# Two-layer encoder trunk: stores to DRAM issued from GpSimd's queue, pad columns written once

## The chip, the cores and the metric

The kernel runs on one core of a Trainium2 chip. The core has five engines that run their own instruction queues: TensorE (PE), VectorE (DVE), ScalarE (ACT), GpSimd (POOL) and SyncE (SP). SyncE computes nothing; here it issues DMAs. The metric is the device time of one execution in microseconds, the median over runs; lower is better.

## What is computed

Two token groups of 512 x 1024 floats go through two layers with shared weights. Layer 0 is a bidirectional RWKV-7 mixer: seven shifted mixes of the normalised input, projections, and per head a recurrence over time, once forward and once backward:

```python
def step(s, inp):
    r_t, w_t, k_t, v_t, a_t, b_t = inp
    sa = jnp.einsum('bhvk,bhk->bhv', s, a_t)
    s = s * w_t[:, :, None, :] + sa[..., None] * b_t[:, :, None, :] + v_t[..., None] * k_t[:, :, None, :]
    return s, jnp.einsum('bhvk,bhk->bhv', s, r_t)
...
y = ys[0] + ys[1]
...
out = y.reshape(bsz, t, D_INNER).astype(xn.dtype) * jax.nn.silu(z)
return out @ w_o
```

Layer 1 is neighbourhood attention on an 8 x 64 grid (16 heads, a window of 8 rows by 16 columns, learned position bias), gated in the same way. Both layers have RMS norms before and after, and a residual sum. All arithmetic is fp32; the kernel splits each fp32 operand of the large products into a high and a low part and multiplies three times.

## The kernel before, in words

Work is laid out as tiles of 128 features x 512 tokens. In order of time:

- **Prelude** (0 to about 150 us in the profile): norms, the shifted mixes, the first projections (`z` and `k` of group 0). Shifted mixes that are needed later are written to DRAM (`dlv`, `dlk`, `dlr`, `dlz`) from a ring of four tiles, `ls`.
- **Scan** (about 150 to 1090 us): the recurrence runs in chunks of 64 tokens, for eight batches of four heads, eight steps each. `prep` makes the operands of a pair of heads, once for each direction `d`: VectorE writes four parts into the tile `ab` (line 851 in `put`), which has one buffer, and line 870 stores it to the DRAM tensor `dab`. `fetch` later loads one step's operands from there into `cab`, and `V` and `X` from `dvt`. `inverse` builds the chunk inverses (`N`, `NA`, `MT`); `near`, `outer` and `step` are the recurrence; `finish` normalises and gates a batch and stores `dy` from the tile `bv`, into which the next half's `bv` is then loaded. Between them `flow` runs the projections of both groups as a stream: weights into `raw` (three buffers), split into `whi` and `wlo`, inputs into `xr`. The results go through `tmp` (five buffers) to DRAM in `column`; the value projection is also transposed into `vs` (two buffers) and stored to `dvt` by two DMAs a tile.
- **Attention** (about 1090 to 1700 us): projections of both groups, `heads`, the output projection. Here q, k, v and gate go through DRAM as well.
- **End**: `last` computes the second group's output and stores it.

In the scan the order on TensorE, VectorE and ScalarE is written out by a planner: `weave` picks the next piece from a set of threads by a clock (`Clock`) that models each engine, SyncE's queue included. The order on SyncE and GpSimd, and everything outside the scan, is set by the framework's scheduler.

All DMAs, loads and stores, are issued by SyncE through two helpers: `load` (line 309) and `save` (line 306), and directly for the output (lines 1389 and 1455). A queue runs in order: an instruction that waits for a semaphore holds back all behind it.

The tile `e1` holds the exponentials of a chunk with a column of ones in front (`d` = 0) or behind (`d` = 1):

```python
e1 = b("e1", (P, NCH, L + 1))
pad = L * d
gps.memset(e1[:, :, pad:pad + 1], 1.0)
e1v, e0v = e1[:, :, 1 - d:L + 1 - d], e1[:, :, d:L + d]
```

`e1` has one buffer, so this memset on GpSimd waits for VectorE's reads of the tile's last use, and ScalarE's exponential waits for the memset. GpSimd's other work is a few memsets: edges of `xn` and `lm` in the prelude, and `MT` (line 946) in `inverse`, 94 instructions in all.

Of the kernel before, what the change touches and what calls it, by code (L numbers as in the profile page):

```python
# [10 lines left out]
F32 = mybir.dt.float32  # L11
# [7 lines left out]
P = 128  # L19
T = 512  # L20
# [3 lines left out]
NCH = 8  # L24
L = 64
# [24 lines left out]
class Clock:  # L50
# [47 lines left out]
    def note(self):  # L98

        ins = self.nc.cur_bb.bb.instructions  # L100
        end = 0.0
        for j in range(self.seen, len(ins)):
            i = ins[j]
            e = self.ENG.get(str(i.engine).split(".")[-1])
            if e is None or not len(i.outs):
                continue
            end = max(end, self.one(e, i))
        self.seen = len(ins)
        return end
# [104 lines left out]
class Trunk:  # L214
# [88 lines left out]

    def save(self, kind, s, p, src):
        self.sp[kind, s, p] = d = self.dram(f"{kind}{s}{p}", src.shape)
        self.nc.sync.dma_start(d, src)

    def load(self, dst, src):
        self.nc.sync.dma_start(dst, src)
# [277 lines left out]
    def column(self, s, kind, p, ps):  # L587

        nc, sp = self.nc, self.sp
        vt, act = nc.vector, nc.scalar  # L590
        first = lambda e: (e, None, lambda c, n=ps.tensor.name: c.at([n]))
        keep, whole = self.clock.keep, ps.tensor.name
        if kind == "z":

            o, th = self.tmp(), self.tmp()
            if s == 0:
                yield first("D")
                vt.tensor_tensor(o, ps, self.rstd0, op=ALU.mult)
                ps = o
            yield "A" if s == 0 else first("A")  # L600
            keep.add(whole)
            act.activation(th, ps, AF.Tanh, scale=0.5)
            yield "D"
            keep.discard(whole)
            vt.scalar_tensor_tensor(o, th, 1.0, ps, op0=ALU.add, op1=ALU.mult)
            self.save("z", s, p, o)
            return
        yield "A", None, lambda c: max(c.at([ps.tensor.name]), min(c.room(("tmp", id(self.main)), self.NTMP), 1e10))
        o = self.tmp()
        if kind == "k":  # L610
            keep.add(whole)
        act.copy(o, ps)
        self.save(kind, s, p, o)
        if kind == "r":
            self.made.add((kind, s, p))
            return
        if kind == "k":
            yield "A"
            keep.discard(whole)
            sq = self.tmp()  # L620
            act.activation(sq, ps, AF.Square, scale=self.vec("kk", p))
            free, room = self.bank()
            yield "P", free, lambda c: max(room(c), c.at([sq.tensor.name]))
            ss = self.p("pm", (2, T))
            nc.tensor.matmul(ss, self.ssel, sq, start=True, stop=True)
            yield "A"
            row = self.tmp((2, T))
            act.copy(row, ss)
            if p == 0:
                sp["ss", s] = self.dram(f"ss{s}", (16, T))  # L630
            self.load(sp["ss", s][2 * p:2 * p + 2], row)
            self.made.add((kind, s, p))
            if p == NP - 1:
                yield "S", None, lambda c: c.at([sp["ss", s].tensor.name])

                rn = self.tmp((P, 64))
                self.load(rn, sp["ss", s].rearrange("a (b c) -> (a b) c", b=8))
                yield "A"
                act.activation(rn, rn, AF.Sqrt)
                yield "D"  # L640
                vt.tensor_scalar(rn, rn, 1e-12, None, op0=ALU.max)
                vt.reciprocal(rn, rn)
                sp["rn", s, 0] = self.dram(f"rn{s}", (16, T))
                self.load(sp["rn", s, 0].rearrange("a (b c) -> (a b) c", b=8), rn)
                self.made.add(("rn", s))
            return

        if p == 0:

            sp["vt", s] = self.dram(f"vt{s}", (4, 2, NCH // 2, 2, L, 2, 2, HD))  # L650
        yield "A"
        back = self.tmp()
        act.copy(back, o[:, ::-1])
        for d in range(2):
            free, room = self.bank()
            yield "P", free, lambda c: max(room(c), c.at([back.tensor.name]))
            vp = self.p("pm")
            for m in range(4):
                nc.tensor.transpose(vp[:, m * P:(m + 1) * P], (back if d else o)[:, m * P:(m + 1) * P], self.ident)
            yield "A", None, lambda c: max(c.at([vp.tensor.name]), c.room(("vs", id(self.main)), self.NVS))  # L660
            vs = self.t("vs", (P, 4, P), self.NVS)
            act.copy(vs, vp.rearrange("p (m c) -> p m c", m=4))
            for j in range(2):
                self.load(
                    sp["vt", s][p // 2, j, :, :, :, d, p % 2].rearrange("m h t c -> t (m h) c"),
                    vs[64 * j:64 * j + 64].rearrange("t m (h c) -> t (m h) c", h=2))
        self.made.add((kind, s, p))
# [90 lines left out]
    def prep(self, s, p):  # L758

        nc, sp = self.nc, self.sp  # L760
        vt, gps, act = nc.vector, nc.gpsimd, nc.scalar
# [38 lines left out]
        for d in range(2):  # L800
# [22 lines left out]
            else:  # L823
                vt.tensor_tensor_scan(cw[:, ::-1], self.scan[1][:, ::-1], u[:, ::-1], 0.0, op0=ALU.mult, op1=ALU.add)
            yield "A"
            e1 = b("e1", (P, NCH, L + 1))
            pad = L * d
            gps.memset(e1[:, :, pad:pad + 1], 1.0)
            e1v, e0v = e1[:, :, 1 - d:L + 1 - d], e1[:, :, d:L + d]
            act.activation(e1v, c3(cw), AF.Exp, scale=-CDEC)  # L830
            e2 = b("u")
            act.activation(e2, cw, AF.Exp, scale=CDEC)


            act.copy(wc[:, d, g] if d == 0 else wc[:, d, g, ::-1], e1[:, :, L - pad])
            ck = max(self.clock.room(("ab", id(self.pp)), 1), 0.0)
            ab = b("ab", (P, NCH, 4, L), 1)

# [28 lines left out]
            yield "D"  # L867
            put(1, mul, c3(kp), c3(e2))
            kps.append(kp)
            self.load(sp["ab", s, pb][:, :, d, g, :].rearrange("c p a -> p c a"), ab.rearrange("p c a t -> p c (a t)"))  # L870

            def gram(ab=ab, d=d):

# [498 lines left out]
    def out1(self, s):  # L1372
        nc = self.nc
# [11 lines left out]
        for k, h in enumerate(hs):  # L1385
            x = self.load(self.t("xr", bufs=self.NXR), self.sp["x1", s, k])
            nc.vector.scalar_tensor_tensor(h, h, self.vec("post1", k), rstd, op0=ALU.mult, op1=ALU.mult)
            (nc.vector if k % 2 else nc.vector).tensor_tensor(h, h, x, op=ALU.add)
            nc.sync.dma_start(self.a["y"][s][k * P:(k + 1) * P, :], h)
            yield  # L1390

    def by_token(self):
# [12 lines left out]
    def last(self):  # L1405
# [27 lines left out]
        for c in range(2):  # L1433
            cs = slice(c * T, c * T + T)
            for m in range(4):
# [12 lines left out]
                if c:  # L1448
# [3 lines left out]
                    vt.reciprocal(r, r)  # L1452
                    for j in range(2):
                        vt.scalar_tensor_tensor(hs[j, m], hs[j, m], r, xt[j], op0=ALU.mult, op1=ALU.add)
                        nc.sync.dma_start(self.a["y"][1][ms, j * T:j * T + T], hs[j, m])


    def stream(self):
# [53 lines left out]
    def scan_phase(self, mid):  # L1512
# [2 lines left out]
        self.mrx = t("mrx", (P, 2, 2, L))  # L1515
        for d in range(2):
            self.nc.vector.tensor_copy(self.mrx[:, d], self.mr[d].unsqueeze(1).broadcast_to([P, 2, L]))
        self.MTb = [t(f"MT{j}", (P, 32, 2, 32)) for j in range(2)]
        self.nM = 0

# [260 lines left out]
```

## Time and profile before

| | |
|---|---|
| median of 3 runs | 1752.39 us (1751.27 to 1755.62) |
| span of the profiled execution | 1748.0 us |
| difference of the two | 4.4 us |
| TensorE busy | 1604.4 us, 92% of the span |
| VectorE busy | 1213.3 us, 69% |
| ScalarE busy | 973.6 us, 56% |
| GpSimd busy | 24.1 us, 1% |
| DMA | 336.26 MB, mean 192 GB/s, of them 105.51 MB written to DRAM |

The profiled execution's own time is its span and what lies around it; of the three runs only the whole time is known, so the span stands beside their median.

How to read it: in the windows, each engine's number is its busy time in the stretch, with the count of instructions. In a table of waits, "A <- B: t, n, m" says that A stood idle for t us in n cases, at most m us, until B was done. SPq is SyncE's queue; a row of its timeline has the start, the time for which the DMA instructions occupied the queue, line, and destination <- source. A bracket at the end of a timeline row gives the idle time before it and what ended it. The DMA list gives the size and the median time from issue to landing.

### The profile page before, as it was taken

What the parts mean: (1) busy time and instruction counts of PE and PEld (TensorE: products, weight loads), DVE (VectorE), ACT (ScalarE), POOL (GpSimd) and SP (SyncE); (2) the same over time, 40 slices, a digit from 0 to 9 for tenths busy, and PEclk for the clock granted to TensorE, in tenths of its full rate; (3) what the DMA queues carried; (4) which work ended last, traced back from release to release, by engine and by line L of the source; (5) the groups of instructions that cost most, each with busy time, mean ns of one, the idle gap of its engine ahead of it and who ended that gap; (6) DMA issues with size and microseconds to landing.
All of it is one profiled execution on the core that took longest, in us unless ns stands there. A gap on an engine that the chain in (4) does not pass through costs nothing.

```text
span 1748.0 us, 46203 instructions
## 1 busy us (share of the span) xinstructions
PE 1604.4 (92%) x18816; PEld 1228.1 (70%) x18816; DVE 1213.3 (69%) x2645; ACT 973.6 (56%) x1964; POOL 24.1 (1%) x94
## 2 busy tenths in 40 slices
PE   7999788998999996898998988999999999999998
PEld 6766665765766674666766676787777788777776
DVE  8976588788888569796888857423556686555564
ACT  5444665666664565666666444333556664555462
POOL 0000000000000000000000000000000000000000
PEclk9989988999999997999999989999999999999999
DMA  5436677685666657777556766554555347545552
GB/s 201 163 115 211 219 266 221 204 269 190 213 198 209 198 172 254 221 213 251 186 187 216 247 200 201 186 204 139 175 184 166 103 132 262 174 155 158 162 175 97
DMA packets 240821, 336.26 MB, mean 192 GB/s; under 512 B 53697, under 2 KB 119361, under 8 KB 240609
## 3 DMA queue, kind: packets, MB, share of 16 engines
q1 hardware_dynamic: 240608, 333.31, 58.7%
q8 instruction: 148, 2.42, 0.6%
q14 instruction: 65, 0.52, 0.1%
HBM read 227.71 MB, written 105.51 MB: 191 GB/s over the span
## 4 chain that ended last, share of the span: by engine, by line
PE 61%; DVE 17%; DMA 8%; ACT 7%; issue 5%; SPq 1%; DVEq 0%; ACTq 0%
PE pg L404 6%; PE pg L405 6%; PE pg L406 6%; PE pm L738 5%; PE pm L739 5%; PE pm L740 5%; PE pm L1331 3%; DVE etmp L928 2%; PE po L1359 2%; PE pt L1346 2%; DVE N L929 2%; PE pf L1030 2%; DVE ab L851 2%; DMA cab<-dab 2%; PE zy L404 1%
## 5 line engine op out<-in xcount | busy, mean ns | idle before, releaser
L738 PE MATMUL pm<-act,whi 128*128 128x512 f32 x608 | 268.6, 442 | 17.9 <-ACT whi L699 8.0
L739 PE MATMUL pm<-act,whi 128*128 128x512 f32 x608 | 246.8, 406 | 19.0 <-DVE act L723 18.7
L740 PE MATMUL pm<-act,wlo 128*128 128x512 f32 x608 | 245.1, 403 | 2.3 <-DVE wlo L701 2.3
L404 PE MATMUL pg<-act,whi 128*128 128x512 f32 x448 | 181.6, 407 | 0.4 <-ACT whi L353 0.4
L405 PE MATMUL pg<-act,whi 128*128 128x512 f32 x448 | 178.4, 398 | 0.0
L406 PE MATMUL pg<-act,wlo 128*128 128x512 f32 x448 | 177.9, 397 | 0.0
L354 DVE TENSOR_TENSOR wlo<-raw,whi 128x512 fp32r<-128x512 f32 x156 | 107.0, 688 | 93.3 <-ACT whi L353 80.5
L353 ACT CAST whi<-raw 128x512 fp32r<-128x512 f32 x156 | 96.2, 618 | 131.6 <-PE pg L405 62.5
L701 DVE TENSOR_TENSOR wlo<-raw,whi 128x512 fp32r<-128x512 f32 x152 | 103.2, 686 | 84.4 <-ACT whi L699 83.1
L738 PEld LDWEIGHTS pm<-act,whi 128*128 128x128 f32 x608 | 117.7, 194 | 54.9 <-ACT whi L699 9.3
L739 PEld LDWEIGHTS pm<-act,whi 128*128 128x128 f32 x608 | 118.3, 195 | 44.9 <-DVE act L723 24.3
L740 PEld LDWEIGHTS pm<-act,wlo 128*128 128x128 f32 x608 | 118.3, 195 | 30.2 <-DVE wlo L701 4.4
L699 ACT CAST whi<-raw 128x512 fp32r<-128x512 f32 x152 | 93.0, 618 | 73.0 <-PE pm L739 55.8
L404 PEld LDWEIGHTS pg<-act,whi 128*128 128x128 f32 x448 | 84.3, 188 | 24.5 <-issue 9.1
L405 PEld LDWEIGHTS pg<-act,whi 128*128 128x128 f32 x448 | 84.3, 188 | 18.4 <-issue 3.5
L406 PEld LDWEIGHTS pg<-act,wlo 128*128 128x128 f32 x448 | 84.2, 188 | 18.2 <-issue 2.2
L929 DVE TENSOR_TENSOR N<-etmp,N 128x30 f32<-128x30 f32 (+14 forms) x240 | 79.8, 332 | 8.2
L1342 ACT ACTIVATE sb<-sb,mx 128x256 f32<-128x256 f32 x128 | 64.1, 502 | 37.6 <-DVE mx L1341 37.1
L928 DVE TENSOR_TENSOR etmp<-N 128x30 f32<-128x30 f32 (+14 forms) x240 | 78.7, 328 | 4.4
L1339 DVE CUSTOM_DVE_ANT_0 sb<-pm,bias 128x256 f32<-128x256 f32 x128 | 50.3, 421 | 45.1 <-PE pm L1331 34.2
L1045 ACT COPY Tm<-pf 128x512 f32<-128x512 f32 x56 | 32.8, 586 | 86.5 <-DVE R L1038 86.5
L1030 PE MATMUL pf<-cab 64*64 64x128 f32 (+1 forms) x2048 | 71.8, 279 | 9.3 <-DMA cab<-dab 6.8
(369 smaller groups left out, 3372.1 us busy)
## 6 DMA issues: line engine op xcount, KB each, us to landing
dab<-ab SPq DMA_DIRECT2D x32, 1024.0 KB, 5.8
cab<-dab SPq DMA_DIRECT2D x64, 512.0 KB, 4.5
raw<-in_w_in_dram SPq DMA_DIRECT2D x128, 256.0 KB, 3.0
bias<-in_rpb_dram SPq DMA_DIRECT2D x32, 384.0 KB, 4.3
raw<-in_w_z_dram SPq DMA_DIRECT2D x32, 256.0 KB, 4.4
dz<-tmp SPq DMA_DIRECT2D x32, 256.0 KB, 2.3
raw<-in_w_k_dram SPq DMA_DIRECT2D x32, 256.0 KB, 3.2
dk<-tmp SPq DMA_DIRECT2D x32, 256.0 KB, 2.2
```

Source lines behind the costliest of these rows:

```text
L353: self.nc.scalar.copy(hi, src)
L354: (eng or self.nc.vector).tensor_tensor(lo, src, hi.bitcast(F32), op=ALU.subtract)
L404: nc.tensor.matmul(ps, hi, x[k][0], start=(k == 0), stop=False)
L405: nc.tensor.matmul(ps, hi, x[k][1], start=False, stop=False)
L406: nc.tensor.matmul(ps, lo, x[k][0], start=False, stop=(k == KT - 1))
L701: nc.vector.tensor_tensor(lo, raw.pop(h), hi.bitcast(F32), op=ALU.subtract)
L738: nc.tensor.matmul(ps, hi[:, at], xh, start=(k == 0), stop=False)
L739: nc.tensor.matmul(ps, hi[:, at], xl, start=False, stop=False)
L740: nc.tensor.matmul(ps, lo[:, at], xh, start=False, stop=(k == KT - 1))
L928: vt.tensor_tensor(tv, N[:, q + 1:, q:q + 1].broadcast_to([P, n, q]), N[:, q:q + 1, :q].broadcast_to([P, n, q]), op=ALU.mult)
L929: vt.tensor_tensor(N[:, q + 1:, :q], tv, N[:, q + 1:, :q], op=ALU.add)
L1030: end = nc.tensor.matmul(f[half(a), h, 0, d, g] if st.last else f[half(a), h, :, d, g], ab[half(h), d, g, 2 * e[d] + a], rt if st.last els ...
```

## The change

Every store to DRAM goes through a new helper `store`, which issues it from GpSimd's queue: `save`, the sums `ss` and `rn`, the transposed values, the operands `ab`, and both outputs. Loads stay on SyncE's. The planner's clock still counts every DMA as SyncE's, whichever engine issues it. The tile `e1` becomes one fixed tile with a column of ones at each end, written once ahead of the scan; the exponentials always lie in columns 1 to 64, and each direction reads a view shifted one way or the other. The 32 memsets in `prep` go.

```diff
-            e = self.ENG.get(str(i.engine).split(".")[-1])
+            e = "S" if "DMA" in type(i).__name__.upper() else self.ENG.get(str(i.engine).split(".")[-1])
...
     def save(self, kind, s, p, src):
         self.sp[kind, s, p] = d = self.dram(f"{kind}{s}{p}", src.shape)
-        self.nc.sync.dma_start(d, src)
+        self.store(d, src)
+
+    def store(self, dst, src):
+        self.nc.gpsimd.dma_start(dst, src)
...
-            self.load(sp["ss", s][2 * p:2 * p + 2], row)
+            self.store(sp["ss", s][2 * p:2 * p + 2], row)
...
-                self.load(
+                self.store(
                     sp["vt", s][p // 2, j, :, :, :, d, p % 2].rearrange("m h t c -> t (m h) c"),
...
-            e1 = b("e1", (P, NCH, L + 1))
-            pad = L * d
-            gps.memset(e1[:, :, pad:pad + 1], 1.0)
-            e1v, e0v = e1[:, :, 1 - d:L + 1 - d], e1[:, :, d:L + d]
+            e1 = self.e1
+            e1v, e0v = e1[:, :, 1:L + 1], e1[:, :, 2 * d:L + 2 * d]
...
-            act.copy(wc[:, d, g] if d == 0 else wc[:, d, g, ::-1], e1[:, :, L - pad])
+            act.copy(wc[:, d, g] if d == 0 else wc[:, d, g, ::-1], e1[:, :, 1 if d else L])
...
-            self.load(sp["ab", s, pb][:, :, d, g, :].rearrange("c p a -> p c a"), ab.rearrange("p c a t -> p c (a t)"))
+            self.store(sp["ab", s, pb][:, :, d, g, :].rearrange("c p a -> p c a"), ab.rearrange("p c a t -> p c (a t)"))
...
-            nc.sync.dma_start(self.a["y"][s][k * P:(k + 1) * P, :], h)
+            self.store(self.a["y"][s][k * P:(k + 1) * P, :], h)
...
+        self.e1 = self.t("e1", (P, NCH, L + 2), 1, F32, self.pp)
+        for pad in (0, L + 1):
+            self.nc.gpsimd.memset(self.e1[:, :, pad:pad + 1], 1.0)
```

(`rn` and the second output change in the same way.) SyncE goes from 1176 rows to 845. The order on TensorE, VectorE and ScalarE is the same in the scan but for a few rows of VectorE and ScalarE at its start; it differs in neighbouring rows in the prelude and in attention.

The first place is SyncE's queue in the scan, in the value projection of group 0, ahead of a load of a step's operands (`cab`; `V`, `X` and `r` are loads too, `dab`, `dvt` and `dks` stores). Before:

```order
L309 DMA V_2749<-dvt_642_2506 128x256
L309 DMA X_2755<-dvt_642_2506 64x2x128
L309 DMA V_2752<-dvt_642_2506 128x256
L309 DMA dab_626_2463<-ab_2733 128x8x256
L309 DMA raw_2791<-in_w_v_dram 128x512
L309 DMA dvt_642_2506<-vs_2799 64x8x64 x2
L309 DMA dvt_642_2506<-vs_2871 64x8x64 x2
L309 DMA cab_441_1698<-dab_466_1778 128x1024
L309 DMA V_2904<-dvt_642_2506 128x256
```

The same place now:

```order
L312 DMA X_2746<-dvt_639_2501 64x2x128
L312 DMA raw_2782<-in_w_v_dram 128x512
L312 DMA V_2743<-dvt_639_2501 128x256
L312 DMA X_2926<-dvt_639_2501 64x2x128
L312 DMA cab_442_1701<-dab_467_1781 128x1024
L312 DMA V_2895<-dvt_639_2501 128x256
L312 DMA r_2972<-dr_525_2020 128x512
```

The operand store and four stores of transposed values no longer stand between the weight load and the `cab` load.

The second place is where those stores stand, around the operand stores of the next pair of heads. On SyncE before (`dv` and `dvt` are the values as projected and transposed, `rb` a load for `prep`):

```order
L306 DMA dv_658_2572<-tmp_2570 128x512
L309 DMA dvt_642_2506<-vs_2593 64x8x64 x2
L309 DMA dvt_642_2506<-vs_2603 64x8x64 x2
L309 DMA dab_626_2463<-ab_2586 128x8x256
L309 DMA raw_2648<-in_w_v_dram 128x512
L309 DMA dvt_642_2506<-vs_2653 64x8x64 x2
L309 DMA X_2755<-dvt_642_2506 64x2x128
L309 DMA X_2935<-dvt_642_2506 64x2x128
L309 DMA rb_2982<-drn_411_1636 64x512
```

On GpSimd now:

```order
L309 DMA dv_655_2567<-tmp_2565 128x512
L309 DMA dvt_639_2501<-vs_2586 64x8x64 x2
L309 DMA dvt_639_2501<-vs_2596 64x8x64 x2
L309 DMA dab_623_2458<-ab_2579 128x8x256
L309 DMA dvt_639_2501<-vs_2646 64x8x64 x2
L309 DMA dv_687_2733<-tmp_2731 128x512
L309 DMA dvt_639_2501<-vs_2736 64x8x64 x2
L309 DMA dvt_639_2501<-vs_2790 64x8x64
L309 DMA dab_623_2458<-ab_2724 128x8x256
```

The stores keep their order among themselves; what stood between them on SyncE, loads, is gone, and the stores follow each other directly on one queue.

More of the change, by code (lines that the diff above doesn't have):

```diff
@@ L643, in column @@
                 sp["rn", s, 0] = self.dram(f"rn{s}", (16, T))
-                self.load(sp["rn", s, 0].rearrange("a (b c) -> (a b) c", b=8), rn)
+                self.store(sp["rn", s, 0].rearrange("a (b c) -> (a b) c", b=8), rn)
                 self.made.add(("rn", s))
@@ L1454, in last @@
                         vt.scalar_tensor_tensor(hs[j, m], hs[j, m], r, xt[j], op0=ALU.mult, op1=ALU.add)
-                        nc.sync.dma_start(self.a["y"][1][ms, j * T:j * T + T], hs[j, m])
+                        self.store(self.a["y"][1][ms, j * T:j * T + T], hs[j, m])
     def stream(self):
```

## The prediction

> **What bounds the kernel now.** I read the page first, then the busy time by stretches, then the chain of waits, and last who waits for DMAs and what the SyncE queue itself waits for. From the page, the engines and the shares of the chain that ended last:
>
> ```profile
> PE 1604.4 (92%) x18816; PEld 1228.1 (70%) x18816; DVE 1213.3 (69%) x2645; ACT 973.6 (56%) x1964; POOL 24.1 (1%) x94
> ...
> PE 61%; DVE 17%; DMA 8%; ACT 7%; issue 5%; SPq 1%; DVEq 0%; ACTq 0%
> ```
>
> The mean hides stages, so the windows come next (us, then busy time of PE, PEld, DVE, ACT, POOL, granted clock, DMA share, GB/s):
>
> ```profile
> 0.00:150.00 150.00, 134.57 (x550) 103.48 (x551) 121.50 (x234) 70.74 (x119) 1.73 (x42) 0.95 0.44 152
> 150.00:1090.00 940.00, 820.89 (x14652) 620.91 (x14651) 733.05 (x1383) 566.80 (x1121) 22.41 (x52) 0.95 0.68 218
> 1090.00:1700.00 610.00, 608.70 (x3413) 471.78 (x3414) 336.38 (x973) 323.22 (x693) 0.00 (x0) 1.00 0.52 171
> 1700.00:1748.00 48.00, 40.19 (x203) 31.96 (x202) 22.32 (x57) 12.81 (x34) 0.00 (x0) 0.95 0.28 94
> ```
>
> From 1090 to 1700 us TensorE is busy for 608.7 of 610 us. Nothing that a queue does there can gain more than 1.3 us. The scan, from 150 to 1090 us, leaves TensorE idle for 119 us; gain and loss are decided there. Who waits for DMAs in the scan (us in total, times, longest), loads first and then stores:
>
> ```profile
> DVE bv L1174 <- DMA bv<-dv: 12.2, 3, 4.7
> ACT act L721 <- DMA xr<-dlv: 10.4, 6, 4.6
> PE pf L1030 <- DMA cab<-dab: 6.8, 5, 3.5
> ACT whi L699 <- DMA raw<-in_w_v_dram: 5.6, 2, 4.9
> DVE ab L851 <- DMA dab<-ab: 3.3, 2, 2.3
> DVE ls L560 <- DMA dlr<-ls: 2.6, 2, 2.2
> ACT vs L662 <- DMA dvt<-vs: 2.4, 1, 2.4
> ```
>
> The loads listed hold an engine for 35 us in all, the stores for 8.3 us. What the SyncE queue waited for in the same window:
>
> ```profile
> SPq L306 <- ACT tmp L612: 31.5, 18, 6.7
> SPq L306 <- ACT tmp L1201: 25.1, 6, 6.7
> SPq L309 <- DMA dy<-bv: 22.3, 12, 3.5
> SPq L309 <- DVE ab L851: 16.2, 14, 2.7
> ```
>
> Three of these four are stores waiting for their producer, with every load behind them waiting too. The third is a load, `bv` or `sz`, that waits until a store has read its buffer or landed.
>
> **The change part by part.**
>
> *SyncE without stores (gain).* The queue's own timeline shows loads straight behind stores, and the chain of waits shows the same loads on the path:
>
> ```profile
> 284.03 5.10 SPq L309 DMA_DIRECT2D dvt<-vs  x4
> 289.23 0.95 SPq L309 DMA_DIRECT2D cab<-dab  x1
> ...
> 377.29 1.72 SPq L309 DMA_DIRECT2D dvt<-vs  x2
> ...
> 379.77 0.38 SPq L309 DMA_DIRECT2D cab<-dab  x1
> ...
> 699.03 2.68 SPq L309 DMA_DIRECT2D dvt<-vs  x4
> ...
> 703.19 1.27 SPq L309 DMA_DIRECT2D k<-dk  x1
> ```
>
> ```profile
> 289.23 4.99 DMA cab<-dab
> ...
> 379.77 4.21 DMA cab<-dab
> ...
> 703.19 6.27 DMA k<-dk
> ```
>
> Without the stores these three could start about 5.2, 2.5 and 4.2 us earlier, 12 us together. That counts each in full and leaves out smaller cases, so I take −12. The ends are 0 (each load meets its next condition, a buffer that TensorE frees) and −29 (these 12 plus the 1% of the span that the chain gives to the SyncE queue, 17 us).
>
> *The operand store on GpSimd (loss).* Each of the 32 `dab<-ab` stores moves 128 x 8 pieces of 1 KB, and `ab` has one buffer, so VectorE may not write the second direction's operands until the first direction's store has landed. Median time from issue to landing, from the page:
>
> ```profile
> dab<-ab SPq DMA_DIRECT2D x32, 1024.0 KB, 5.8
> ...
> dvt<-vs SPq DMA_DIRECT2D x64, 128.0 KB, 3.4
> ...
> dy<-bv SPq DMA_DIRECT2D x16, 256.0 KB, 3.4
> ```
>
> VectorE's timeline shows the reuse, in the first and the last of the sixteen pairs (last write of the first direction, first write of the second):
>
> ```profile
> 200.46 0.69 DVE L851 TENSOR_TENSOR ab<-kp,u 128x512 f32<-128x512 f32 x1
> ...
> 206.56 0.69 DVE L851 TENSOR_TENSOR ab<-r,e 128x512 f32<-128x512 f32 x1 [1.02 <-DMA dab<-ab]
> ...
> 916.17 0.69 DVE L851 TENSOR_TENSOR ab<-kp,u 128x512 f32<-128x512 f32 x1
> ...
> 923.77 0.70 DVE L851 TENSOR_TENSOR ab<-r,e 128x512 f32<-128x512 f32 x1 [0.54 <-ACT e L830]
> ```
>
> From the end of one write to the start of the next the sixteen gaps are 5.1 to 10.9 us; less the 3.3 us of waiting in them, 4.4, 5.1, 5.3, 5.6, 5.8, 5.9, 6.4, 6.6, 6.9, 7.1, 8.2, 9.0, 9.9, 10.4, 10.8 and 10.9. A store of 5.8 us just fits. If it takes L, VectorE stalls by the sum of L minus gap: 5.8 us for L = 6.3, 11 for 7, 26 for 8.5, 78 for 12.3.
>
> No row shows a store issued by GpSimd, so I bound what GpSimd adds by its memsets:
>
> ```profile
> L1527 POOL MEMSET MT<- 128x2048 f32 x2 | 3.6, 1816 | 29.5 <-DMA raw<-in_w_r_dram 29.5
> L493 POOL MEMSET xn<- 128x1 f32 x16 | 1.1, 98 | 0.3 <-POOLq L1768 0.3
> ```
>
> One element per partition costs (1816 − 98) / 2047 = 0.84 ns. If describing a piece costs as much, 1024 pieces take 0.9 us; eight times that is 6.9 us, my outer bound. The landing time includes SyncE's issue of about 0.4 us, so L lies between 6.3 and 12.3. I take L = 8.5, four times the element price (3.4 us), less the 0.4 and a little overlap. The stall grows by 26 − 3.3 = 23 us. VectorE is in order and busy for 733 of 940 us, and the scan's `R`, `AK` and `S` steps stand behind the stalled write; TensorE has other products to do meanwhile. I let half through: +11.5, with ends of +1 and +75 (all of 78 − 3.3).
>
> *`vt` stores ahead of an operand store.* A `dvt<-vs` store has 64 x 8 = 512 pieces, 1.7 us at the same price, where the four at 699.03 took SyncE 2.68 us together. In GpSimd's new order four of them stand ahead of an `ab` store in the value projection: 6.8 us instead of 2.7, so 4 us later, about twice, half of it through: +4, ends 0 and +12.
>
> *Loads that wait for a store.* `dy<-bv` has 128 pieces, some 0.5 us more at that price; twelve waits of SyncE and the three of VectorE on `bv` grow by this: +2. The `ls` and `vs` buffers, 5 us of waiting now, wait somewhat longer: +3. Both have 0 as one end and, if every such wait doubles, +10 as the other.
>
> *The end.* The last output stores, from the queue's timeline:
>
> ```profile
> 1740.10 5.12 SPq L1455 DMA_DIRECT2D out_dram<-oa  x4
> ```
>
> Issue ends at 1745.2 and the span at 1748.0; that landing has no cover, so a slower issue counts in full: +1, ends 0 and +3.
>
> *The pad columns.* 32 memsets of `e` on GpSimd go, and with them a hop from VectorE over GpSimd to ScalarE. GpSimd appears nowhere on the chain, so 0. Left in place, they would have stood ahead of stores. The `MT` memsets stay and now stand between stores. The order of TensorE, VectorE and ScalarE is unchanged in the scan but for a few rows at its start; it changes a little in attention, where TensorE is full: 0, give or take 2.
>
> Sum: −12 + 11.5 + 4 + 2 + 3 + 1 = +9.5 us on a span of 1748.0. The profiled execution is 4.4 us below the median of 1752.39, which I put down to what lies around the span, so the forecast is 1752.4 + 9.5 = 1762 us.
>
> **The rivals.** *Cheap issue, faster.* If GpSimd adds under 1 us, L is at most 6.3. Then the operand store costs +1, the bursts nothing, the rest +1, and the relief of −12 stands: about −10, or 1742 us; with the wider relief 1725. It decides from L = 7 down, where the stall is 11 us and half of its growth 4. For it: 0.84 ns per element, and the 73 us of SyncE's waiting in the three store rows above. Against it: ten of the sixteen gaps are under 7.2 us, so there is little room. Chance 0.30. The Trainium skill speaks for this side: "DMA: Bandwidth & Descriptors", "Latency and other measured facts", gives the first byte at about 0.6 us from SyncE and 1 us from GpSimd; by that, as an estimate, L would be 6.2 and the sum about −10. No run here shows it yet.
>
> *Nothing to see.* A relief of 5 to 15 us meets costs of the same size; within 0.3%, 5.3 us, which is about what a measurement of this kernel can tell from no change. 1752 us, chance 0.15.
>
> *VectorE starves GpSimd.* If GpSimd can describe pieces only while VectorE is idle, 22% of the scan, 2.7 us become 12.3, L is 18, and the stall 16 x 18 − 118 = 170 us; half of it gives +85, about 1835 us. For it: VectorE's load. Against: GpSimd's large memsets in the scan (count, then shortest, median and longest ns) keep one steady time beside that load:
>
> ```profile
> L946 POOL MEMSET MT<- x16: 942/945/951, 297.0 to 1013.1; 32x1024 f32 x16
> ```
>
> Chance 0.05. A box of the Trainium skill, "SBUF — State Buffer", section "SBUF: two separate sides", warns of this trap for stores from GpSimd, but for VectorE's fast one-input copies; the scan's operations listed above have two inputs, so the rule would need a wider reach to matter here, and no row decides that.
>
> **How the numbers follow.** The forecast has 0.45; a heavier version of it, L near 12 with half through (+38 in place of 11.5, some 1795 us with bursts doubled), 0.05; the starved case 0.05; no difference 0.15; faster 0.30. Slower is 0.55. The range runs from 1736 (inside the cheap case, leaving out its far end) to 1800 (the heavy version), and leaves out the starved case. Cases of both signs hold most of the chance; the likeliest alone spans 1757 to 1785.
>
> **What would show it.** Right: VectorE's wait for `dab<-ab` at its operand writes rises from 3.3 to some 26 us; the landing of `dab<-ab` rises to 8 or more; SyncE's waits for `tmp` producers vanish; idle TensorE time between 150 and 1090 us grows from 119 to about 128 us; 1090 to 1700 stays as it is. Wrong: landing stays near 6 us and TensorE's idle time in the scan falls, or the waits move to places with no store in them, such as `MT`.

## The result, and the profile after

The changed kernel takes 1782.16 us (median of four runs, 1780.83 to 1783.13), the kernel before beside it 1751.83 us: a ratio of 1.0161, 95% interval 1.0140 to 1.0181. That is 28 to 30 us slower, inside the range given, but three times the 9.5 us that the sum gave. The span of the profiled execution grew from 1748.0 to 1779.1 us. What lies around a span is 1.7 to 2.2 us in every run on record (1780.83 against 1779.1 here); of the 4.4 us that the prediction put down to it, the rest is the difference between one execution and another.

Where the 31 us lie is read from the same operations in both traces: the last write of `bv`, which closes the scan, and the last head's exponentials, `sb`, near the end of attention. Before, then after:

```profile
1125.31 0.69 DVE L1174 TENSOR_TENSOR bv<-pm,bv 128x512 f32<-128x512 f32 x1 [1.31 <-DMA bv<-dv]
1704.05 0.19 ACT L1342 ACTIVATION_READ_ACCUMULATOR sb<-sb,mx 128x1 f32 x1
1743.45 1.42 DVE L1454 SCALAR_TENSOR_TENSOR oa<-oa,st,tmp 128x512 f32<-128x512 f32 x2
```

```profile
1147.77 0.69 DVE L1175 TENSOR_TENSOR bv<-pm,bv 128x512 f32<-128x512 f32 x1 [1.71 <-DMA bv<-dv]
1731.38 0.19 ACT L1343 ACTIVATION_READ_ACCUMULATOR sb<-sb,mx 128x1 f32 x1
1769.83 1.42 DVE L1455 SCALAR_TENSOR_TENSOR oa<-oa,st,tmp 128x512 f32<-128x512 f32 x2
```

The scan ends 22.5 us later. Attention adds 4.9 us (27.3 at `sb`), of which VectorE wins 0.9 back by its last operation (1771.25 against 1744.87, 26.4). From there to the end of the span it takes 7.8 us instead of 3.1: 4.7 more. 22.5 + 4.9 − 0.9 + 4.7 is the 31 us. Each trace is one execution: in a second trace of the changed kernel (further down) the scan ends 28.2 us late and attention adds 5.1.

The scan's and attention's stretches of the trace after, with the boundary between them and the end moved by the 22 us (columns as in the prediction):

```profile
150.00:1112.00 962.00, 827.85 (x14647) 623.93 (x14645) 732.02 (x1382) 566.04 (x1120) 164.76 (x252) 0.94 0.66 213
1112.00:1722.00 610.00, 607.27 (x3397) 468.81 (x3398) 333.75 (x958) 321.07 (x685) 43.91 (x81) 1.00 0.52 170
```

TensorE's idle time in the scan is 134 us where it was 119; in the 610 us of attention it is 2.7 where it was 1.3, so that stage kept its shape until its last heads.

The 15 us more of idle time are not all of the scan's 22. The other 7 are TensorE's own work: 827.85 us where it was 820.89, for as many matmuls (14647 and 14652), at a mean granted clock of 0.94 where it was 0.95. It is so over all executions on record: the mean clock of the whole execution has a median of 0.959 over the changed kernel's ten, and of 0.966 over the 103 of the kernel before that ran beside the experiments. There too a lower clock goes with more time (1741.2 us at 0.971, 1766.2 at 0.958, on one chip). Whether the longer waits lower the clock, or something else does, no run here separates.

Who waits for DMAs in the scan, from the table of waits after:

```profile
DVE bv L1175 <- DMA bv<-dv: 17.4, 6, 5.5
DVE ab L852 <- DMA dab<-ab: 15.8, 7, 3.7
PE pf L1031 <- DMA cab<-dab: 12.3, 6, 3.1
ACT act L724 <- DMA xr<-dlv: 9.5, 3, 6.1
DVE rb L792 <- DMA k<-dk: 8.0, 1, 8.0
```

The wait of VectorE for the operand store, `dab<-ab`, went from 3.3 to 15.8 us as foretold in kind. But the loads that SyncE was to bring earlier are hardly waited for less: `bv` 17.4 us (before 12.2), `cab` 12.3 (6.8), `xr` 9.5 (10.4). Of these only `bv` is beyond what executions differ by: with the pad columns alone (below), in the time of the kernel before, `cab` has 12.3 us as well and `bv` 7.8. The 8.0 us for `k`, one wait at the scan's start, are new (1.2 before). SyncE's own queue shows why nothing need have come free:

```profile
SPq L312 <- DVE wlo L704: 212.7, 73, 11.3
SPq L312 <- PE zy L1119: 95.9, 41, 7.3
SPq L312 <- DVE etmp L929: 45.0, 26, 6.6
SPq L312 <- DVE act L726: 41.2, 20, 5.7
```

Its waits for the producers of `tmp` are gone, but a queue with less to issue reaches its next blocked load sooner: it now waits 213 us for buffers of weights (`wlo` reads the last of a `raw` tile) where the table of before has 98.0, and 96 where that has 51.3 for TensorE's `zy`.

What a store costs on GpSimd, the groups of its instructions (count, then busy us and mean ns of one), and the landing times from the page:

```profile
L309 POOL DMA_DIRECT2D dvt<-vs x64 | 44.2, 695 | 112.7 <-ACT vs L665 102.4 <-ACT whi L702 8.9 <-issue 1.3
L309 POOL DMA_DIRECT2D dab<-ab x32 | 28.9, 902 | 103.8 <-DVE ab L852 95.7 <-DVE etmp L929 5.2 <-DVE st L1164 3.0
...
L309 POOL DMA_DIRECT2D dy<-bv x16 | 8.7, 541 | 87.6 <-DVE bv L1186 86.8 <-DVE etmp L929 0.7
```

```profile
dab<-ab POOLq DMA_DIRECT2D x32, 1024.0 KB, 7.0
...
dvt<-vs POOLq DMA_DIRECT2D x64, 128.0 KB, 3.8
...
dy<-bv POOLq DMA_DIRECT2D x16, 256.0 KB, 4.3
```

541 ns for 128 pieces, 695 for 512 and 902 for 1024 lie on a line of 0.49 us and 0.40 ns a piece. The operand store lands after 7.0 us instead of 5.8, `y` after 4.3 instead of 3.4. The numbers of before are medians of few stores: on SyncE's queue the trace tells the landing of 4 of the 32 operand stores and of 6 of the 16 of `y`, on GpSimd's that of all. In the kernel with only the operand stores put back on SyncE (below) it tells 26 of 32, with a median of 5.9; in the changed kernel the same 26 land later by a median of 0.9 us. The two directions also differ. Where only the first direction's operand stores are issued from GpSimd they land after 6.1 us, where only the second's are, after 7.4. The rows of these three kernels:

```profile
dab<-ab SPq DMA_DIRECT2D x32, 1024.0 KB, 5.9
```

```profile
dab<-ab POOLq DMA_DIRECT2D x16, 1024.0 KB, 6.1
```

```profile
dab<-ab POOLq DMA_DIRECT2D x16, 1024.0 KB, 7.4
```

One trap of the page: the chain that ended last now reads "PE 47%; issue 22%" where it had PE 61%. It was followed back along GpSimd's queue, which stands idle between two stores; in attention that says nothing about what bounds the time.

### The profile page after: what moved, and what is told of

It reads as the page before. It is cut to its first block, busy times and chain, and to the rows that moved or that the text cites. A ratio compares the mean times of both kernels' runs of the same rounds, so it can differ in the third digit from the quotient of the medians.

```text
span 1779.1 us, 46342 instructions
## 1 busy us (share of the span) xinstructions
PE 1615.2 (91%) x18816; PEld 1232.2 (69%) x18816; DVE 1213.9 (68%) x2645; ACT 973.9 (55%) x1964; POOL 235.9 (13%) x422
## 4 chain that ended last, share of the span: by engine, by line
PE 47%; issue 22%; DVE 13%; DMA 9%; ACT 5%; POOL 3%; SPq 0%; POOLq 0%; DVEq 0%; ACTq 0%
PE pm L741 4%; PE pg L407 4%; PE pg L408 4%; PE pg L409 4%; PE pm L742 4%; PE pm L743 4%; PE pm L1332 2%; DMA cab<-dab 2%; DMA dab<-ab 2%; PE pf L1031 2%; DVE etmp L929 2%; DVE N L930 1%; PE po L1360 1%; PE pt L1347 1%; PE zy L407 1%
## 5 line engine op out<-in xcount | busy, mean ns | idle before, releaser
L741 PE MATMUL pm<-act,whi 128*128 128x512 f32 x608 | 272.9, 449 | 10.8 <-ACT wc L836 2.8
L742 PE MATMUL pm<-act,whi 128*128 128x512 f32 x608 | 250.3, 412 | 21.7 <-DVE act L726 21.4
L743 PE MATMUL pm<-act,wlo 128*128 128x512 f32 x608 | 249.2, 410 | 4.1 <-DVE wlo L704 3.9
L742 PEld LDWEIGHTS pm<-act,whi 128*128 128x128 f32 x608 | 120.7, 199 | 50.0 <-DVE act L726 27.8
L741 PEld LDWEIGHTS pm<-act,whi 128*128 128x128 f32 x608 | 120.1, 198 | 48.1 <-ACT whi L702 6.3
L1031 PE MATMUL pf<-cab 64*64 64x128 f32 (+1 forms) x2048 | 71.0, 275 | 17.5 <-DMA cab<-dab 12.3
```

The lines of the kernel that those rows point to most:

```text
L741: nc.tensor.matmul(ps, hi[:, at], xh, start=(k == 0), stop=False)
L742: nc.tensor.matmul(ps, hi[:, at], xl, start=False, stop=False)
L743: nc.tensor.matmul(ps, lo[:, at], xh, start=False, stop=(k == KT - 1))
L1031: end = nc.tensor.matmul(f[half(a), h, 0, d, g] if st.last else f[half(a), h, :, d, g], ab[half(h), d, g, 2 * e[d] + a], rt if st.last els ...
```

## The experiments

**Theory A**: GpSimd's stores land later, and whoever waits for a store pays: the reuse of `ab`, the tile `bv`, the loads that read a stored tensor, and the end. **Rivals**: the pad columns or a new order cost; SyncE's loads, freed of stores, hold each other back (B); or the end is late for another reason. Ratios are to the kernel before on the same chip, with 95% intervals; 0.1% is 1.75 us.

**Pad columns alone.** All stores back on SyncE.

```diff
     def store(self, dst, src):
-        self.nc.gpsimd.dma_start(dst, src)
+        self.nc.sync.dma_start(dst, src)
```

> All stores go back to SyncE's queue; the fixed tile with its two columns of ones stays. Theory A (GpSimd's stores land later, 7.0 us instead of 5.8 us for the operand store, and the places that wait for a store lose; the pad columns are worth nothing): 1752 us, as before, within 3 us. Rival (the fixed tile or the order that it gives costs part of the 30 us): 1757 us or more.

Measured: 1.0001 (0.9983 to 1.0019). The fixed tile costs and gains nothing. All kernels below that start from "stores on SyncE" contain it.

**Changed kernel, operand stores back on SyncE.**

```diff
-            self.store(sp["ab", s, pb][...], ab...)
+            self.load(sp["ab", s, pb][...], ab...)
```

> The changed kernel with only the 32 operand stores put back on SyncE. Theory A: VectorE's wait for them falls from 15.8 us to about 3, TensorE's for the loads behind them from 17 to 8; some 15 of the 30 us come back, 1767 us. Theory B (what costs is that loads of weights, which wait for a buffer, now stand directly ahead of the scan's loads on SyncE, whatever stores are gone): nearly nothing comes back, 1778 to 1782 us, or worse, since the operand stores then wait behind those loads.

Measured: 1.0118 (1.0099 to 1.0138), 1774 us, between the two: 7 to 8 of the 28 us come back, half of what theory A had. VectorE's wait for the store fell to 1.5 us.

**Only the operand stores on GpSimd.**

```diff
     def store(self, dst, src):
-        self.nc.gpsimd.dma_start(dst, src)
+        self.nc.sync.dma_start(dst, src)
...
-            self.store(sp["ab", s, pb][...], ab...)
+            self.nc.gpsimd.dma_start(sp["ab", s, pb][...], ab...)
```

> The kernel before with its fixed tile, only the 32 operand stores on GpSimd. Theory A: the operand store's landing alone costs some 15 us, 1767 us, with VectorE's wait for it near 15 us. Theory B: the queue of SyncE is nearly as before, 1752 to 1756 us. If GpSimd's queue is late because other stores stand ahead of the operand store, not because its stores land later: also 1752 to 1756 us, with landing still near 7 us but few waits.

Measured: 1.0079 (1.0057 to 1.0101), 14 us, as theory A had it in time. Its table of waits, however, shows VectorE waiting 8.1 us for the store, not 15, and TensorE 9.5 us for `V`; so the two halves were tried apart.

**Second direction's, and first direction's, operand stores on GpSimd** (all else on SyncE).

```diff
-            self.store(sp["ab", s, pb][...], ab...)
+            (gps if d else nc.sync).dma_start(sp["ab", s, pb][...], ab...)
```

```diff
-            self.store(sp["ab", s, pb][...], ab...)
+            (nc.sync if d else gps).dma_start(sp["ab", s, pb][...], ab...)
```

> Only the operand stores of the second direction on GpSimd (16 of the 32), everything else on SyncE. The next write of the operand tile comes 30 us or more after them, so their landing blocks no write. If the 11 us of the operand stores come from the reuse of the tile between the two directions: no loss here, 1753 us within 3 us. If they come from the loads of operands that read the stored tensor, or from the mixed queues as such: half or more of it stays, 1758 to 1766 us.

> Only the operand stores of the first direction on GpSimd, everything else on SyncE: the counterpart of the run with the second direction, which cost 4.3 us of the 13.9 that both cost. If the reuse of the tile between the directions is the larger part: 9 to 10 us longer than before, 1763 us, VectorE's wait for the store at 8 us. If the parts do not add up that way (each half costs 4 to 5 us, and both together more): 1758 us.

Measured: second direction 1.0024 (1.0006 to 1.0041), 4 us; first direction 1.0051 (1.0025 to 1.0078), 9 us. Together 13, the 14 of both. VectorE's wait at the operand write, with the pad columns alone and then with the first direction on GpSimd:

```profile
DVE ab L852 <- DMA dab<-ab: 5.0, 3, 2.4
```

```profile
DVE ab L852 <- DMA dab<-ab: 14.3, 7, 4.2
```

9.3 us more waiting in this trace, and 9 us more time over twelve executions (4 to 14 by the interval): most of this stall is paid, perhaps all. Where only the second direction is on GpSimd that wait is 6.0 us, so its 4 us, where reuse of the tile alone would have cost nothing, come from elsewhere; readers of `dab` and SyncE's changed queue are both left, and not told apart. The direct test, a second buffer for `ab`, was not run.

**Only the transposed values (`vt`) on GpSimd.**

```diff
     def store(self, dst, src):
-        self.nc.gpsimd.dma_start(dst, src)
+        self.nc.sync.dma_start(dst, src)
...
-                self.store(
+                self.nc.gpsimd.dma_start(
                     sp["vt", s][p // 2, j, :, :, :, d, p % 2].rearrange("m h t c -> t (m h) c"),
```

> The kernel before with its fixed tile, only the 64 stores of transposed values on GpSimd. With all stores but the operands' on GpSimd, the scan was 11 us longer, the end of attention 5 us, the end 5 us. If the value stores are what costs in the scan (four of them in a row on a queue that takes 0.7 us for each, ahead of loads that read them): 1763 us. If it is the saves of projections and of y: 1752 us, or 1747 us if SyncE gains from the 64 stores that it no longer issues.

Measured: 1.0025 (1.0001 to 1.0049), 4 us: between the expectations. With 64 stores fewer on SyncE there is no net gain. Beside the same operations of the kernel before, VectorE's in this trace run some 4 us ahead from 580 to 700 us and 2 to 6 behind from 800 on, past the second group's value projection; with the pad columns alone they differ by up to 3 us, so one trace only hints at a gain that is lost again.

**Only the saves on GpSimd.** Operand stores, `vt` and outputs through `load`, in the changed kernel.

```diff
-            self.store(sp["ab", s, pb][...], ab...)
+            self.load(sp["ab", s, pb][...], ab...)
...
-                self.store(
+                self.load(
                     sp["vt", s][...]
...
-            self.store(self.a["y"][...], h)
+            self.load(self.a["y"][...], h)
```

> The changed kernel with the operand stores, the stores of transposed values and the outputs on SyncE; on GpSimd stay the saves of whole tiles and the two small sums. If the saves are what costs in the scan: the scan 11 us longer, the end of attention 5 us, 1768 us. If the transposed values are: only the end of attention, 1757 us. If neither alone costs, but the fact that SyncE's queue is empty of stores (loads wait at its head for a buffer, others behind them): between, 1759 to 1764 us here and with the values alone.

Measured: 1.0060 (1.0040 to 1.0079), 10.5 us. Which saves, the next two tell.

**Only `y` on GpSimd; only z, v, r, k and ks on GpSimd.**

```diff
-        self.store(d, src)
+        (self.nc.gpsimd if kind == "y" else self.nc.sync).dma_start(d, src)
```

```diff
-        self.store(d, src)
+        (self.nc.gpsimd if kind in ("z", "v", "r", "k", "ks") else self.nc.sync).dma_start(d, src)
```

> Only the 16 stores of y on GpSimd. The saves together cost 10.5 us, and VectorE's wait for the tile that y is stored from and the next value loaded into rose from 7.8 to 20.8 us with them. If the stores of y are the cause: 6 to 10 us longer, 1760 us, that wait at 14 us or more. If it is the saves of projections or of attention: 1753 us, the wait at 8 to 12 us as before.

> Only the scan's saves of z, v, r, k (both groups) and of ks on GpSimd, the stores that hold SyncE's queue longest while they wait for their producers (some 60 us in all) and whose readers come much later. If taking them away relieves the loads behind them, as the prediction had it: 4 to 12 us faster, 1741 to 1749 us. If the relief is worth nothing: 1753 us within 3. If later landing of these saves costs: 1757 us or more.

Measured: `y` 1.0025 (1.0005 to 1.0045), 4 us, less than the 6 to 10 expected, with VectorE's wait for `bv` as expected; with the pad columns alone, then with `y` on GpSimd:

```profile
DVE bv L1175 <- DMA bv<-dv: 7.8, 3, 4.0
```

```profile
DVE bv L1175 <- DMA bv<-dv: 19.7, 5, 6.2
```

Twelve more microseconds of waiting. The wait is the doing of these stores: it is 17 to 21 us in all eight traces with `y` on GpSimd, and 7 to 14 in the ten with `y` elsewhere. How much of it is absorbed stays open: the loss is 4 us by the ratio (1 to 8 by the interval), but the very execution that was traced is 8.8 us longer than that with the pad columns alone (spans of 1757.1 and 1748.3). The projections' saves: 1.0007 (0.9991 to 1.0022). They are the stores that held SyncE longest, and taking them off it gains nothing that can be told (between 1.6 us of gain and 3.9 of loss).

**Attention's saves back on SyncE; the outputs back on SyncE; both** (from the changed kernel).

```diff
-        self.store(d, src)
+        (self.load if kind in ("q1", "k1", "v1", "z1") else self.store)(d, src)
```

```diff
-            self.store(self.a["y"][s][k * P:(k + 1) * P, :], h)
+            self.load(self.a["y"][s][k * P:(k + 1) * P, :], h)
...
-                        self.store(self.a["y"][1][ms, j * T:j * T + T], hs[j, m])
+                        self.load(self.a["y"][1][ms, j * T:j * T + T], hs[j, m])
```

> The changed kernel with attention's saves (q, k, v, gate; 64 stores) back on SyncE. In the three traces with these saves on GpSimd, the last head's weights come 4 to 5 us later beside what stands before attention; in the one with only the operand stores there, 2 us. If the saves are the cause: 4 to 5 us less than the changed kernel, 1777 us. If it is the order of attention's work, which the scheduler sets anew: no difference, 1781 to 1783 us.

> The changed kernel with the 16 stores of both outputs put back on SyncE. From the last VectorE operation to the end of the span went 3.1 us before and 7.8 us after: if the issue on GpSimd is what ends last, 4 to 5 us come back, 1777.5 us. If the difference lies in when the last rows are ready, and not in their store: 1781 to 1783 us.

> The changed kernel with attention's saves and both outputs back on SyncE, so that only the stores up to the end of the scan are on GpSimd. If the terms of attention (0.6% when it alone was put back) and of the outputs (0.5%) add up: 0.5% over the kernel before, 1762 us. If they overlap, and the scan's loss is what the traces show (19 to 22 us): 1.1%, 1773 us.

Measured: 1.0101 (1.0074 to 1.0127), 1.0113 (1.0091 to 1.0135) and, for both, 1.0109 (1.0080 to 1.0137). Each alone brings back 8 to 11 us of the 28, more than the 4 to 5 expected. The changed kernel again, on the chip of the last:

> The changed kernel as it is, on the same chip as the run beside it. If the first comparison (four runs) holds: 1.6% over the kernel before, 1782 us. If the parts, which add up to over 2%, are right and the first comparison was low: 1790 us.

Measured: 1.0152 (1.0119 to 1.0185). So the first comparison holds, and the two terms do not add up; together they are worth 0.4 to 0.5%, 7 to 9 us. In the trace of the kernel with both back, the scan and attention stand as follows:

```profile
1147.70 0.69 DVE L1175 TENSOR_TENSOR bv<-pm,bv 128x512 f32<-128x512 f32 x1 [2.84 <-DMA bv<-dv]
1726.31 0.19 ACT L1343 ACTIVATION_READ_ACCUMULATOR sb<-sb,mx 128x1 f32 x1
1765.68 1.41 DVE L1455 SCALAR_TENSOR_TENSOR oa<-oa,st,tmp 128x512 f32<-128x512 f32 x2
```

22.4 us late at the end of the scan and 22.3 at the last head: attention's 4.9 us are gone. From the last VectorE operation (1767.09) to the end of the span (1770.3) it takes 3.2 us: the end's 4.7 are gone too. How the 7 to 9 us split between attention and the end, the intervals do not tell. Nor are the saves the whole of attention's part: between the end of the scan and the last head, the five traces with them on GpSimd add 4.9 to 6.1 us to the kernel before, but among those with them on SyncE some add nothing and some up to 3.5 (the one with only the operand stores on GpSimd; 3.2 where only these saves were put back).

**ScalarE's queue instead of GpSimd's.** The saves that ScalarE produces, and `vt`, from its own queue; the rest on SyncE.

```diff
-        self.store(d, src)
+        (self.nc.scalar if kind in ("v", "r", "k", "q1", "k1", "v1") else self.nc.sync).dma_start(d, src)
...
-                self.store(
+                nc.scalar.dma_start(
                     sp["vt", s][p // 2, j, :, :, :, d, p % 2].rearrange("m h t c -> t (m h) c"),
```

> The kernel before with its fixed tile; the saves that ScalarE produces (v, r, k, and q, k, v of attention) and the stores of transposed values are issued from ScalarE's own queue, all others from SyncE's. These stores never wait there, since their producer is ScalarE. If the time is lost by GpSimd's later landing: no loss here, 1742 to 1754 us (a gain if SyncE's relief is worth anything, less ScalarE's time for 160 issues). If it is lost because SyncE's loads then stand at the head of their queue and hold each other back: a loss of about 10 us, 1762 us, with any queue.

Measured: 1.0143 (1.0119 to 1.0167), 25 us, worse than any expectation, and no test of B: landing was short (`vt` 2.9 us), but the issue stands in ScalarE's own program, between its copies:

```profile
282.44 0.57 ACT L665 COPY vs<-pm 128x512 f32<-128x512 f32 x1
283.04 1.30 ACTq L667 DMA_DIRECT2D dvt<-vs  x2
284.38 0.37 ACT L893 COPY Gd<-pf 64x256 f32<-64x256 f32 x1 [1.37 <-PE pm L662]
...
285.56 0.58 ACT L665 COPY vs<-pm 128x512 f32<-128x512 f32 x1
286.18 2.10 ACTq L667 DMA_DIRECT2D dvt<-vs  x2
```

That is a median of 0.64 us of ScalarE for each of the 64 (0.58 to 2.31), some 41 us, in the scan's value projections, where ScalarE feeds the others; each of the 96 saves takes another 0.33. That this is what costs the 25 us was not tested apart.

**Weight loads off SyncE, alone and with the projections' saves.** To test theory B, the scan's weight loads go to GpSimd's queue; stores stay on SyncE (or, in the second kernel, z, v, r, k and ks go too).

```diff
-                    raw[2 * c + j] = self.load(self.t("raw", (P, self.WP), self.NRAW), src[...])
+                    raw[2 * c + j] = self.loadw(self.t("raw", (P, self.WP), self.NRAW), src[...])
...
+    def loadw(self, dst, src):
+        self.nc.gpsimd.dma_start(dst, src)
+        return dst
```

> All stores on SyncE, as in the kernel before; instead, the scan's 152 loads of weights (raw, three buffers) are issued from GpSimd's queue. With the stores gone from SyncE its queue waited most of all at weight loads for a buffer (213 us in the scan, against 98 before), with every other load behind them. If that is what ate the relief: SyncE's waits for wlo vanish, cab, V, k, r start earlier, 4 to 12 us faster, 1742 to 1750 us. If no load behind the head of SyncE's queue is what the scan waits for: 1753 us within 3. If the weights themselves, which land later from GpSimd, hold ScalarE: 1757 us or more.

> The same with the scan's saves of z, v, r, k and ks on GpSimd too, whose move alone cost nothing that can be told (1755 us). If relief of SyncE counts once the weight loads are off it: faster than the run with the weights alone, 1738 to 1748 us. If the weight loads now wait behind saves on GpSimd's queue, or no relief counts: 1753 us or more.

Measured: 1.0019 (1.0005 to 1.0032) and 1.0064 (1.0047 to 1.0082). SyncE's longest waits in the scan, with the pad columns alone and then with the weights on GpSimd:

```profile
SPq L312 <- DVE wlo L704: 100.9, 58, 7.7
SPq L312 <- PE zy L1119: 51.4, 30, 4.8
SPq L309 <- ACT tmp L615: 34.7, 16, 6.7
```

```profile
SPq L316 <- PE zy L1123: 67.6, 33, 6.9
SPq L309 <- ACT tmp L619: 67.4, 25, 9.9
```

The 101 us at weight loads are gone and the next waits have grown instead; with the saves gone as well, TensorE still waits 11.3 us for `cab`, with the pad columns alone 12.3. So theory B finds no support either: with the stores that held SyncE longest, with the weights, or with both off its queue, the scan is not shorter. These are net times; a gain that is lost again on GpSimd's queue is not excluded. No version beat the kernel before.

## Why the prediction was wrong

The direction was right, and so was the place of the largest stall; the size was not, by 20 us. Step by step:

- **SyncE's relief, −12: the step that failed.** It took three loads in the chain that ended last as loads that an engine waited for, and added up the delays of their issue. The trace of before shows no engine waiting for two of them (rows below). Behind the `cab` load of 289.23, landed at 294.22, the chain goes on in SyncE's own queue, and the next matmul that reads a `cab` at all begins at 324.38. The `k` load of 703.19, landed at 709.46, is first read at 722.39, without a wait. Only for the load of 379.77 did TensorE stand idle, 2.33 us, and in the changed kernel it stands idle 2.26 us at the same place. So at most 2.3 of the 12 us were there to be won, and they were not. The first load did come earlier: it begins at 289.29 after, while the operand write ahead of it, 273.91 in the chain of before, begins at 281.30, so it came 7 us earlier in its place, and no engine had use for that. The runs agree: the stores that held the queue longest taken off alone (1.0007), `vt` alone (a loss), weights instead (a loss), no net gain from any. The prediction's other end, 0, was the right value. With it the scan's terms make +20.5, where the scan's stores together cost 19.
- **The operand store, +11.5: near the 14 measured, by luck.** L was taken as 8.5 us, with 3.4 for issue; it is 7.0, with 0.90, and only 6.1 for the first direction, whose landing is the one waited for. The table of gaps gave 11 us of stall for 7 and 5.8 for 6.3; measured were 8.1 (all operand stores), 14.3 (the first direction's) and 15.8 (the whole change), so one median is a poor stand-in for sixteen landings. "Half let through" was too little: 9.3 us of added wait went with 9 us of time. And the second direction, which the working left out because nothing reuses the tile soon after it, cost 4.
- **`vt`, +4:** 4 measured with these stores alone, though there they stand ahead of no operand store, so the mechanism was not the one named. In the changed kernel the named one is seen too: nine of the 32 operand stores start right behind a `vt` store, up to 2.0 us after their tile was written. In the rows below `ab` is written by 273.56, and its store starts at 273.99, right behind a `vt` store of 0.70.
- **`dy` and `bv`, +2:** 4 measured. A landing 0.9 us longer in the whole change; alone, 12 us more of waiting. Why a delay of 0.9 us grew to so much in the five waits counted there stays open. **`ls` and `vs`, +3:** VectorE's wait for `ls` on `dlr` fell from 2.6 to 0.9 and ScalarE's for `vs` rose from 2.4 to 3.9 us: about nothing.
- **The end, +1, and attention, 0: 7 to 9 together.** The working counted the issue of the last stores and not their landing, and took a full TensorE in attention as cover up to the last head.
- **TensorE's own time, in no term:** 7 of the scan's 22 us in the traces above, at the lower clock.
- **Pad columns, 0:** 1.0001.

The rows of before for the first point, from the chain and from the timelines of TensorE and VectorE, and the same wait of TensorE after:

```profile
294.24 0.02 SPq L309
```

```profile
324.38 0.63 PE L1005 MATMUL zy<-cab 64*64 64x64 f32 x16
384.11 1.16 PE L1030 MATMUL pf<-cab 64*64 64x128 f32 x32 [2.33 <-DMA cab<-dab]
722.39 0.74 DVE L789 SCALAR_TENSOR_TENSOR rb<-k,cv,rb 128x512 f32<-128x512 f32 x1
```

```profile
390.90 1.10 PE L1031 MATMUL pf<-cab 64*64 64x128 f32 x32 [2.26 <-DMA cab<-dab]
```

More rows for the first and third point, from the timelines of VectorE, GpSimd and SyncE after:

```profile
272.87 0.69 DVE L852 TENSOR_TENSOR ab<-kp,u 128x512 f32<-128x512 f32 x1
281.30 0.69 DVE L852 TENSOR_TENSOR ab<-r,e 128x512 f32<-128x512 f32 x1 [0.55 <-DMA dab<-ab]
```

```profile
273.30 0.70 POOL L309 DMA_DIRECT2D dvt<-vs  x1 [1.25 <-issue]
273.99 0.89 POOL L309 DMA_DIRECT2D dab<-ab  x1
```

```profile
289.29 1.57 SPq L312 DMA_DIRECT2D cab<-dab  x1
```

Measured one by one, the scan's parts (14, 4, 4 and 1 us) make 23 where the scan's stores together cost 19 (1.0109): a little overlap, within the intervals. With 7 to 9 for the rest that is the whole.

The rival of a cheap issue had its condition met and still failed: under 1 us of GpSimd's time a store, with a median landing of 7.0 us, its own point of decision; without the relief nothing is left to be fast. The Trainium skill ("DMA: Bandwidth & Descriptors", "Latency and other measured facts") gives the first byte at about 0.6 us from SyncE and 1 us from GpSimd, 0.4 us apart. Here `y` and the operand store landed 0.9 us or more later from GpSimd, and the measurement decides; an L of 6.2 by that page is still near the 6.1 of the first direction. The starved GpSimd is out: in the scan, with VectorE busy for 732 of 962 us, its 32 operand stores took 894 ns at least, 902 in the middle and 927 at most.

```profile
L309 POOL DMA_DIRECT2D dab<-ab x32: 894/902/927, 202.3 to 948.1; - x32
```

The Trainium skill also says ("Perfetto Trace Analysis", "DMA Optimizations") that it may make sense to give loads and stores an issuing engine each, above all with loops or control flow. For this kernel no run bears it out: the whole split costs 1.5 to 1.6%, and its cheapest part gains nothing.

## What to carry to other kernels

A queue that waits is not a loss until an engine waits for what stands behind it: before counting a freed queue as a gain, take for each load the wait that an engine shows for it, and ask what the queue's head will wait for next. A DMA in the chain that ended last is not yet such a wait: look for the bracket at the engine's own row. For a store moved to a slower issuer, list who waits for its landing: the next write of its one buffer, a load of the same tile, the end of the program; here about 1 us more at each of sixteen stores cost 9 us at the buffer and 4 at the load. Moving the stores that nobody soon waits for cost nothing that could be told, and gained nothing either.

## What the runs showed of the hardware

- A store issued by GpSimd took 0.49 us of that engine and 0.40 ns a piece (541, 695 and 902 ns for 128, 512 and 1024 pieces), and did not slow down beside a busy VectorE (894 to 927 ns); its landing came 0.9 to 1.2 us later than SyncE's for `y` and the operands by the medians above, and 0.9 us for the 26 operand stores whose landing both traces tell.
- ScalarE spent 0.64 us of its own time (the median) to issue a store of 512 pieces (two took 1.30 us in one row above, 2.10 in another).
- With the outputs on GpSimd the time from the last VectorE operation to the end of the span was 7.8 us in both traces of the changed kernel, 9.9 with the operand stores back on SyncE and 4.2 with attention's saves back; with the outputs on SyncE it was 3.1 to 3.4 in all fourteen traces. GpSimd's two last issues, 1.2 us together, explain a part of that; what the rest is, and why it varies so, no row says.
- The same bytes travelled in fewer packets, though the total time was longer. Before, then after:

```profile
DMA packets 240821, 336.26 MB, mean 192 GB/s; under 512 B 53697, under 2 KB 119361, under 8 KB 240609
```

```profile
DMA packets 170262, 336.27 MB, mean 189 GB/s; under 512 B 21120, under 2 KB 54016, under 8 KB 170048
```
